# Casting the opening loads inside the DMA: matmul, GELU, matmul on one Trainium2 core

## The chip, the cores and the metric

The kernel runs on one core of a Trainium2 chip. A core has a matrix engine (TensorE, PE in the profile, with PEld for its weight loads), a vector engine (VectorE, DVE), a scalar engine (ScalarE, ACT), GpSimd (POOL) and a queue engine (SyncE, SP). Each engine works through its own list of instructions in order and waits for the others only through semaphores. Two lists issue loads here: SP's, whose transfers copy a type as it is, and POOL's, whose transfers may change the type on the way (float32 in the device memory, bf16 in the on-chip memory, SBUF). Both use the same 16 DMA engines. Matmul results land in PSUM, of which the kernel uses eight banks of 128 x 512 float32.

The metric is the device time of one execution in microseconds. Before the change the median of 13 executions is 124.84 us (124.44 to 125.33).

## The reference

```python
m, k, n, p = 1024, 1024, 2048, 1024      # a: m x k, b: k x n, c: n x p, all float32

def reference(a, b, c):
    h = np.matmul(a, b)
    h = 0.5 * h * (1 + np.tanh(np.sqrt(2 / np.pi) * (h + 0.044715 * h ** 3)))
    return np.matmul(h, c).astype(np.float32)
```

## The kernel before

The first product is computed transposed, so that its result can serve as the weights of the second. It is cut into 16 tiles of 128 columns of b (index t) and into two halves of 512 rows of a (index h). For one tile and one half eight matmuls (index k, 128 rows of b each) add up in one PSUM bank: weights are a 128 x 128 block of b, the moving operand is aT[h][:, k, :], 512 turned rows of a. ScalarE applies GELU from PSUM into the tiles hq (line 119). The second product is done in seven products of half matrices in place of eight (line 246), with sums and differences of the halves made by VectorE beforehand (s1, s2, s3, t1, t2, t3). The order of all work is the order in which the program is written.

What is loaded, and where:

- The opening block is 768 columns of b (tiles t = 0 to 5, W0) and the first half of a. SP loads both as float32: a_st (line 76; two slices of 128 columns, then three pairs) and b_st (line 82; eight slices, one for each k, 128 rows of 3072 bytes). SP's order is a slice, b slice, a slice, b slice, a pair, two b slices, and so on.
- For each k the loop at line 105 casts a_st to bf16 (ab, line 107, VectorE), turns it with four transposes on TensorE (line 110) into a bank of tpool, copies that to aT[0] (line 111, VectorE), casts b_st to b_lo with two ScalarE instructions (line 113), and issues the six matmuls of slice k - 1 (line 102).
- Tiles 6 to 9 (W1, 512 columns) come with two loads on POOL (load_b, line 126), each four slices of k, cast to bf16 on the way into b_lo. Ahead of them stands the gate (line 91), a copy of one column on POOL that reads slice 5 of b_st, so POOL issues nothing before that slice has landed. Here k is the outer loop: 32 matmuls (line 134) into four banks.
- Tiles 10 to 15 come into b_hi with four POOL loads, two k halves for 384 columns (W2) and two for the next 384. They run with t outside and k inside (mm1, line 143).
- The second half of a comes with four POOL loads (line 155), each 128 rows, cast to bf16. turn (line 158) makes eight transposes into a bank of tpool and one copy to aT[1] (line 163). turn(0) stands behind tile 13, turn(1) to turn(3) behind tile 14.
- c comes in eight POOL loads (line 188).

tpool has two banks, ppool six. The four tiles t1 take the buffers of a_st, the eight tiles t2 those of b_st (lines 195 and 196), and the partial results u2 those of the a1 slices.

Loads issued on POOL share eight semaphores in turn, so a load's issue waits until the eighth load before it on this queue has landed.

Of the kernel before, what the change touches and what calls it, by code (L numbers as in the profile page):

```python
# [19 lines left out]
def kernel(ctx, tc, a, b, c, out):  # L20
# [7 lines left out]
    H = 512  # L28
    N0 = 6
    W0 = N0 * 128  # L30
    N1 = 4
    W1 = N1 * 128

# [6 lines left out]
    keep = ctx.enter_context(tc.tile_pool(name="keep", bufs=1))  # L40
    astage = ctx.enter_context(tc.tile_pool(name="astage", bufs=4))
    abf = ctx.enter_context(tc.tile_pool(name="abf", bufs=4))
    b0stage = ctx.enter_context(tc.tile_pool(name="b0stage", bufs=8))
    opool = ctx.enter_context(tc.tile_pool(name="opool", bufs=4))
    ppool = ctx.enter_context(tc.tile_pool(name="ppool", bufs=6, space=PSUM))
    tpool = ctx.enter_context(tc.tile_pool(name="tpool", bufs=2, space=PSUM))

# [11 lines left out]
    def bcols(k0, kn, n0, w):  # L59
        if n0 < WB:  # L60
            return b_lo[:, k0:k0 + kn, ds(n0, w)]
        return b_hi[:, k0:k0 + kn, ds(n0 - WB, w)]

    def bt(k, t):
        return bcols(k, 1, t * 128, 128)[:, 0, :]
# [5 lines left out]

    a_st, b_st = {}, {}

    def load_a0(k, n):
        st = astage.tile([128, 4, 256], F32, name="a_st")
        nc.sync.dma_start(out=st[:, :, 0:n * 128], in_=av[:, 0:4, ds(k * 128, n * 128)])  # L76
        for i in range(n):
            a_st[k + i] = st[:, :, ts(i, 128)]

    def load_b0(k):  # L80
        st = b0stage.tile([128, W0], F32, name="b0_st")
        nc.sync.dma_start(out=st, in_=bv[:, k, 0:W0])  # L82
        b_st[k] = st

    gate = consts.tile([128, 1], F32, name="gate")
    for k, n in ((0, 1), (1, 1), (2, 2), (4, 2), (6, 2)):
        load_a0(k, n)
        for i in range(n):
            load_b0(k + i)

    nc.gpsimd.tensor_copy(gate, b_st[5][:, 0:1])
    g = consts.tile([128, 1], F32, name="g")
    nc.scalar.activation(g, warm[:, 0:1], AF.Gelu_apprx_tanh)
    wps = tpool.tile([128, H], F32, name="pt")
    for _ in range(10):
        nc.tensor.matmul(wps, warm[:, 0:128], warm, start=True, stop=True)

    ps = [ppool.tile([128, H], F32, name="ps") for _ in range(N0)]

    def mm0(k):  # L100
        for t in range(N0):
            nc.tensor.matmul(ps[t], bt(k, t), aT[0][:, k, :],  # L102
                             start=(k == 0), stop=(k == KT - 1))

    for k in range(KT):
        ab = abf.tile([128, 4, 128], BF16, name="ab")
        nc.vector.tensor_copy(ab, a_st[k])  # L107
        pt = tpool.tile([128, H], BF16, name="pt")
        for j in range(4):
            nc.tensor.transpose(pt[:, ts(j, 128)], ab[:, j, :], ident)  # L110
        nc.vector.tensor_copy(aT[0][:, k, :], pt)
        for i in range(2):
            nc.scalar.activation(b_lo[:, k, ts(i, W0 // 2)], b_st[k][:, ts(i, W0 // 2)], AF.Copy)  # L113
        if k > 0:
            mm0(k - 1)
    mm0(KT - 1)

    def gelu(t, h, p):
        nc.scalar.activation(hq[h][t // NH][:, t % NH, :], p, AF.Gelu_apprx_tanh)  # L119

    for t in range(N0):
        gelu(t, 0, ps[t])


    def load_b(k0, kn, n0, w):
        nc.gpsimd.dma_start(out=bcols(k0, kn, n0, w), in_=bv[:, k0:k0 + kn, ds(n0, w)])

    ps = [(tpool if t < 2 else ppool).tile([128, H], F32, name="pt" if t < 2 else "ps")
          for t in range(N1)]
    for k in range(0, KT, 4):  # L130
        load_b(k, 4, W0, W1)
        for i in range(4):
            for t in range(N1):
                nc.tensor.matmul(ps[t], bt(k + i, N0 + t), aT[0][:, k + i, :],  # L134
                                 start=(k + i == 0), stop=(k + i == KT - 1))
    for t in range(N1):
        gelu(N0 + t, 0, ps[t])


    def mm1(t, h):  # L140
        p = ppool.tile([128, H], F32, name="ps")
        for k in range(KT):
            nc.tensor.matmul(p, bt(k, t), aT[h][:, k, :],  # L143
                             start=(k == 0), stop=(k == KT - 1))
        gelu(t, h, p)

    W2 = 384
    for n0 in range(W0 + W1, N, W2):
# [9 lines left out]
    def turn(j):  # L158
        ab = a1[j]
        pt = tpool.tile([128, KT, 128], BF16, name="pt")  # L160
        for k in range(KT):
            nc.tensor.transpose(pt[:, k, :], ab[:, ts(k, 128)], ident)  # L162
        nc.vector.tensor_copy(aT[1][:, :, ts(j, 128)], pt)  # L163

    for t in range(N0 + N1, NT):
        mm1(t, 0)
        if t == NT - 3:
            turn(0)
        if t == NT - 2:
            turn(1)  # L170
            turn(2)
            turn(3)

# [20 lines left out]

    t1 = [astage.tile([128, 2, H], F32R, name="t1", tag="a_st") for _ in range(4)]
    t2 = [b0stage.tile([128, 1, H], F32R, name="t2", tag="b0_st") for _ in range(8)]
    s1 = keep.tile([128, NH, H], F32R, name="s1")
# [3 lines left out]

    def sum_t2(t):
        nc.vector.tensor_tensor(t2[t], c22[:, t:t + 1, :], t1[t // 2][:, t % 2:t % 2 + 1, :], op=SUB)

# [3 lines left out]
    for t in range(NT):  # L208
        mm1(t, 1)
        if 3 <= t < 7:  # L210
            sum_t1(t - 3)
        if 6 <= t < 10:
            sum_t2(2 * (t - 6))
            sum_t2(2 * (t - 6) + 1)
        if t == WB // 128:
            t3 = keep.tile([128, NH, H], F32R, name="t3", tag="B0")
        if t >= NH + 1:
            sum_s1(t - NH - 1)
        if WB // 128 <= t < WB // 128 + 4:
            i = t - WB // 128  # L220
            nc.vector.tensor_tensor(t3[:, ts(i, 2), :], c22[:, ts(i, 2), :], c12[:, ts(i, 2), :], op=SUB)
# [15 lines left out]

    def sum_t4(t):
        nc.vector.tensor_tensor(t2[t], t2[t], c21[:, t:t + 1, :], op=SUB)

# [8 lines left out]
    def whole(x):  # L249
        return lambda t: x[:, t, :]  # L250

    def halves(x):
        return lambda t: x[t // 4][:, t % 4, :]

    def pairs(x):
        return lambda t: x[t // 2][:, t % 2, :]

    def ones(x):
        return lambda t: x[t][:, 0, :]

# [26 lines left out]
    for j in R:  # L287
        p = bank()
        prod(p, halves(s2), ones(t2), j)
        nc.vector.tensor_tensor(u2[j], p, u2[j], op=ADD)  # L290
# [5 lines left out]
    for j in R:  # L296
        p = bank()
        prod(p, whole(s1), pairs(t1), j)
        combine(4 + j, 1, p, u3[:, j, :])
        nc.vector.tensor_tensor(u2[j], p, u2[j], op=ADD)  # L300
        sum_t4(2 * j)
        sum_t4(2 * j + 1)
    for j in R:
# [3 lines left out]
    for j in R:  # L307
        p = bank()
        prod(p, whole(h22), ones(t2), j)
        combine(4 + j, 0, p, u3[:, j, :], op=SUB, swap=True)  # L310
# [36 lines left out]
```

## Time and profile before

| What | Value |
|---|---|
| median of 13 executions | 124.84 us (124.44 to 125.33) |
| the profiled execution: its own time | 124.44 us |
| the profiled execution: its span | 122.7 us |
| PE busy | 114.8 us (94%), 555 instructions |
| DVE busy | 65.2 us (53%) |
| ACT busy | 29.6 us (24%) |
| POOL busy | 21.4 us (17%) |
| queue 0 (POOL's loads, "software_dynamic") | 7968 packets, 8.91 MB |
| queue 1 (SP's loads and stores, "hardware_dynamic") | 6240 packets, 9.44 MB |
| read from device memory, written to it | 20.97 MB, 4.19 MB |

The span runs from the first to the last instruction of the profiled execution; its own time is 1.7 us longer, for what lies around the program. The profile page cuts the span into 40 slices of 3.07 us. "Busy tenths" give the busy share of each engine in a slice, PEclk the clock granted to TensorE, GB/s what the DMA engines wrote: a load that casts float32 to bf16 writes half of what it reads. The chain of waits is followed backwards from the last instruction, at each step to what released it. In a timeline a row gives start, duration, engine, line, operation, output and input, count, and in brackets the idle time before it and what ended that.

### The profile page before, as it was taken

How to read it: one execution, taken by the hardware profiler on the slowest of the kernel's cores; microseconds unless marked ns; L12 is line 12 of the kernel's file. 1: busy time of each engine (PE TensorE's matmuls, PEld its weight loads, DVE VectorE, ACT ScalarE, POOL GpSimd, SP SyncE). 2: the span in 40 equal slices, each digit the busy share in tenths (PEclk: the TensorE clock that was granted, in tenths of full speed). 3: DMA queues.
4: the chain of work that ended last, by engine and by line, in shares of the span. 5: the costliest groups of instructions: out<-in, count | busy, mean ns of one | idle time of the engine just before them, and what ended most of it. 6: DMA issues, size and time to landing. Idle time of an engine off the chain costs nothing.

```text
span 122.7 us, 1436 instructions
## 1 busy us (share of the span) xinstructions
PE 114.8 (94%) x555; PEld 67.2 (55%) x562; DVE 65.2 (53%) x94; ACT 29.6 (24%) x54; POOL 21.4 (17%) x26
## 2 busy tenths in 40 slices
PE   6759989999998999999999999999999999999990
PEld 2224444444456444444444444468888888888860
DVE  0223543000014200007999999999769999964440
ACT  4054445806331133233332333000000000000000
POOL 2000099133440310000000000996000000000000
PEclk9977999999999999999999999999999999999999
DMA  2799999999999999996000000000600023353433
GB/s 92 213 368 380 377 303 198 206 201 202 211 206 206 322 397 234 206 206 100 0 3 0 5 0 0 0 0 25 232 0 0 5 86 120 137 199 143 171 143 114
DMA packets 14213, 18.43 MB, mean 150 GB/s; under 512 B 768, under 2 KB 9728, under 8 KB 14208
## 3 DMA queue, kind: packets, MB, share of 16 engines
q0 software_dynamic: 7968, 8.91, 39.3%
q1 hardware_dynamic: 6240, 9.44, 21.7%
q8 instruction: 4, 0.07, 0.2%
q14 instruction: 1, 0.01, 0.0%
HBM read 20.97 MB, written 4.19 MB: 205 GB/s over the span
## 4 chain that ended last, share of the span: by engine, by line
PE 82%; DMA 12%; DVE 1%; SPq 1%; issue 1%; DVEq 0%
PE ps L246 41%; PE ps L143 31%; DMA a_st<-in_a_dram 12%; PE ps L102 3%; PE ps L134 3%; PE pt L134 3%; PE pt L162 1%; DVE aT L163 1%; PE pt L110 1%; DVE ab L107 0%; SPq L82 0%; DVE ot L316 0%; SPq L76 0%; DVEq L107 0%
## 5 line engine op out<-in xcount | busy, mean ns | idle before, releaser
L119 ACT ACTIVATE h<-ps 128x512 fp32r<-128x512 f32 (+1 forms) x30 | 17.3, 601 | 27.5 <-PE ps L143 25.2
L143 PE MATMUL ps<-aT,b_hi 128*128 128x512 bf16 x93 | 21.2, 379 | 0.2
L143 PE MATMUL ps<-aT,b_lo 128*128 128x512 bf16 x79 | 17.4, 379 | 0.1
L143 PEld LDWEIGHTS <-b_hi 128*128 128x128 bf16 x96 | 9.3, 98 | 10.8
L246 PE MATMUL ps<-t,s 128*128 128x512 f32 x64 | 15.0, 392 | 0.0
L246 PE MATMUL ps<-t,h 128*128 128x512 f32 x64 | 14.8, 389 | 0.0
L246 PE MATMUL ps<-c,h 128*128 128x512 bf16 (+1 forms) x71 | 14.1, 355 | 0.1
L286 POOL COPY lk<-u 128x512 f32<-128x512 f32 x1 | 7.9, 7892 | 33.4 <-ACT u L279 33.4
L246 PEld LDWEIGHTS ps<-t,s 128*128 128x128 f32 x64 | 12.0, 188 | 2.6
L246 PEld LDWEIGHTS ps<-t,h 128*128 128x128 f32 x64 | 12.0, 188 | 2.5
L200 DVE TENSOR_TENSOR t<-c,c 128x1024 fp32r<-128x1024 bf16 x4 | 4.7, 1222 | 15.7 <-DMA c<-in_c_dram 15.4
L143 PEld LDWEIGHTS <-b_lo 128*128 128x128 bf16 x80 | 7.8, 98 | 9.4
L102 PE MATMUL ps<-aT,b_lo 128*128 128x512 bf16 x47 | 12.9, 414 | 0.1
L163 DVE COPY aT<-pt 128x1024 bf16<-128x1024 bf16 x4 | 2.7, 688 | 18.0 <-PE pt L162 17.9
L246 PEld LDWEIGHTS <-h 128*128 128x128 bf16 x72 | 6.9, 98 | 7.1 <-issue 0.3
L113 ACT ACTIVATE b_lo<-b_st 128x384 bf16<-128x384 f32 x16 | 7.5, 515 | 10.0 <-DMA b_st<-in_b_dram 9.8
L188 POOL DMA_DIRECT2D c<-in_c_dram x8 | 6.0, 745 | 12.4 <-DMA b_hi<-in_b_dram 5.7
L269 DVE TENSOR_TENSOR ot<-ps,u 128x512 f32<-128x512 f32 x11 | 7.3, 683 | 1.1 <-PE ps L246 1.1
L246 PE MATMUL ps<-c,s 128*128 128x512 f32 x32 | 7.4, 389 | 0.0
L102 PEld LDWEIGHTS <-b_lo 128*128 128x128 bf16 x48 | 4.8, 107 | 4.7 <-issue 1.3
L107 DVE CAST ab<-a_st 128x512 bf16<-128x512 f32 x8 | 3.7, 464 | 6.3 <-DMA a_st<-in_a_dram 6.3
L246 PEld LDWEIGHTS ps<-c,s 128*128 128x128 f32 x32 | 6.0, 188 | 1.2
(37 smaller groups left out, 89.8 us busy)
## 6 DMA issues: line engine op xcount, KB each, us to landing
out_dram<-ot SPq DMA_DIRECT2D x15, 256.0 KB, 2.0
b_st<-in_b_dram SPq DMA_DIRECT2D x8, 384.0 KB, 8.5
c<-in_c_dram POOLq DMA_DIRECT2D x6, 512.0 KB, 15.0
c<-in_c_dram POOLq DMA_DIRECT2D x2, 1024.0 KB, 15.0
a_st<-in_a_dram SPq DMA_DIRECT2D x3, 512.0 KB, 9.0
b_hi<-in_b_dram POOLq DMA_DIRECT2D x4, 384.0 KB, 11.4
b_lo<-in_b_dram POOLq DMA_DIRECT2D x2, 512.0 KB, 6.9
ab<-in_a_dram POOLq DMA_DIRECT2D x4, 256.0 KB, 14.1
```

The source lines that it names most:

```text
L102: nc.tensor.matmul(ps[t], bt(k, t), aT[0][:, k, :], start=(k == 0), stop=(k == KT - 1))
L107: nc.vector.tensor_copy(ab, a_st[k])
L113: nc.scalar.activation(b_lo[:, k, ts(i, W0 // 2)], b_st[k][:, ts(i, W0 // 2)], AF.Copy)
L119: nc.scalar.activation(hq[h][t // NH][:, t % NH, :], p, AF.Gelu_apprx_tanh)
L134: nc.tensor.matmul(ps[t], bt(k + i, N0 + t), aT[0][:, k + i, :], start=(k + i == 0), stop=(k + i == KT - 1))
L143: nc.tensor.matmul(p, bt(k, t), aT[h][:, k, :], start=(k == 0), stop=(k == KT - 1))
L163: nc.vector.tensor_copy(aT[1][:, :, ts(j, 128)], pt)
L188: nc.gpsimd.dma_start(out=dst[:, t:t + 4, :], in_=cv[:, r * NH + t:r * NH + t + 4, ts(q, H)])
L200: nc.vector.tensor_tensor(t1[i], c12[:, ts(i, 2), :], c11[:, ts(i, 2), :], op=SUB)
L246: nc.tensor.matmul(p, lhs(t)[:, ts(j, 128)], rhs(t)[:, q], start=(t == 0), stop=(t == NH - 1))
L269: nc.vector.tensor_tensor(ot, u if swap else p, p if swap else u, op=op)
L286: nc.gpsimd.tensor_copy(last_keep, last)
```

## The change

All loads but the first two a slices go to POOL and are cast inside the DMA. The opening order on POOL is b slice 0, b slice 1, then for each pair of k an a pair and two b slices; b slices go straight into b_lo, so b0stage and ScalarE's casts are gone, and VectorE casts only the first two a slices. The gate goes. The loads of b_lo's second block and of b_hi follow on the same queue, and b_hi now comes in two loads of 768 columns (one for each k half), since W2 is the whole rest.

In the opening loop the transposes and the copy of slice k + 1 stand between the third and fourth matmul of slice k. All transposes of the opening go through one PSUM bank cut in two (pts); ppool has seven banks, tpool one. The turns of the second half of a take banks of ppool and are placed inside tiles: turn(0) behind tile 13, turn(1) after four matmuls of tile 14, turn(2) behind it, turn(3) after four matmuls of tile 15. t1 and t2 get buffers of their own; t2 is four tiles of 128 x 1024, and the sums on it are done in four instructions in place of eight. NB equals N0, so the loop over range(NB, N0) is empty.

```diff
     N0 = 6
+    NB = 6
...
+    KG = 4
...
-    astage = ctx.enter_context(tc.tile_pool(name="astage", bufs=4))
+    astage = ctx.enter_context(tc.tile_pool(name="astage", bufs=2))
     abf = ctx.enter_context(tc.tile_pool(name="abf", bufs=4))
-    b0stage = ctx.enter_context(tc.tile_pool(name="b0stage", bufs=8))
...
-    ppool = ctx.enter_context(tc.tile_pool(name="ppool", bufs=6, space=PSUM))
-    tpool = ctx.enter_context(tc.tile_pool(name="tpool", bufs=2, space=PSUM))
+    ppool = ctx.enter_context(tc.tile_pool(name="ppool", bufs=7, space=PSUM))
+    tpool = ctx.enter_context(tc.tile_pool(name="tpool", bufs=1, space=PSUM))
...
-    def load_a0(k, n):
-        st = astage.tile([128, 4, 256], F32, name="a_st")
-        nc.sync.dma_start(out=st[:, :, 0:n * 128], in_=av[:, 0:4, ds(k * 128, n * 128)])
...
-    def load_b0(k):
-        st = b0stage.tile([128, W0], F32, name="b0_st")
-        nc.sync.dma_start(out=st, in_=bv[:, k, 0:W0])
-        b_st[k] = st
-
-    gate = consts.tile([128, 1], F32, name="gate")
-    for k, n in ((0, 1), (1, 1), (2, 2), (4, 2), (6, 2)):
-        load_a0(k, n)
-        for i in range(n):
-            load_b0(k + i)
-
-    nc.gpsimd.tensor_copy(gate, b_st[5][:, 0:1])
+    def load_b(k0, kn, n0, w):
+        nc.gpsimd.dma_start(out=bcols(k0, kn, n0, w), in_=bv[:, k0:k0 + kn, ds(n0, w)])
+
+    a_bf = {}
+    a_st = []
+    for k in range(2):
+        st = astage.tile([128, 4, 128], F32, name="a_st")
+        nc.sync.dma_start(out=st, in_=av[:, 0:4, ts(k, 128)])
+        a_st.append(st)
+    load_b(0, 1, 0, W0)
+    load_b(1, 1, 0, W0)
+    for k in range(2, KT, 2):
+        st = abf.tile([128, 4, 256], BF16, name="ab", tag="ab1")
+        nc.gpsimd.dma_start(out=st, in_=av[:, 0:4, ds(k * 128, 256)])
+        for i in range(2):
+            a_bf[k + i] = st[:, :, ts(i, 128)]
+            load_b(k + i, 1, 0, W0)
...
-    for k in range(KT):
-        ab = abf.tile([128, 4, 128], BF16, name="ab")
-        nc.vector.tensor_copy(ab, a_st[k])
-        pt = tpool.tile([128, H], BF16, name="pt")
+    def turn0(k):
+        if k < 2:
+            ab = abf.tile([128, 4, 128], BF16, name="ab0", bufs=2)
+            nc.vector.tensor_copy(ab, a_st[k])
+        else:
+            ab = a_bf[k]
+        pt = pts[:, k % 2, :]
         for j in range(4):
             nc.tensor.transpose(pt[:, ts(j, 128)], ab[:, j, :], ident)
         nc.vector.tensor_copy(aT[0][:, k, :], pt)
-        for i in range(2):
-            nc.scalar.activation(b_lo[:, k, ts(i, W0 // 2)], b_st[k][:, ts(i, W0 // 2)], AF.Copy)
-        if k > 0:
-            mm0(k - 1)
-    mm0(KT - 1)
+
+    turn0(0)
+    for k in range(KT):
+        for t in range(NB):
+            nc.tensor.matmul(ps[t], bt(k, t), aT[0][:, k, :],
+                             start=(k == 0), stop=(k == KT - 1))
+            if t == 2 and k + 1 < KT:
+                turn0(k + 1)
...
-    def mm1(t, h):
+    def mm1(t, h, between={}):
         p = ppool.tile([128, H], F32, name="ps")
         for k in range(KT):
             nc.tensor.matmul(p, bt(k, t), aT[h][:, k, :],
                              start=(k == 0), stop=(k == KT - 1))
+            for x in between.get(k, ()):
+                turn(x)
         gelu(t, h, p)
...
-    W2 = 384
+    W2 = N - W0 - W1
     for n0 in range(W0 + W1, N, W2):
         for k in range(0, KT, 4):
             load_b(k, 4, n0, W2)
...
     def turn(j):
-        ab = a1[j]
-        pt = tpool.tile([128, KT, 128], BF16, name="pt")
+        pt = ppool.tile([128, KT, 128], BF16, name="pt", tag="ps")
         for k in range(KT):
-            nc.tensor.transpose(pt[:, k, :], ab[:, ts(k, 128)], ident)
+            nc.tensor.transpose(pt[:, k, :], a1[j][:, ts(k, 128)], ident)
         nc.vector.tensor_copy(aT[1][:, :, ts(j, 128)], pt)
 
+    turns = {NT - 3: {7: [0]}, NT - 2: {3: [1], 7: [2]}, NT - 1: {3: [3]}}
     for t in range(N0 + N1, NT):
-        mm1(t, 0)
-        if t == NT - 3:
-            turn(0)
-        if t == NT - 2:
-            turn(1)
-            turn(2)
-            turn(3)
+        mm1(t, 0, turns.get(t, {}))
...
-    t1 = [astage.tile([128, 2, H], F32R, name="t1", tag="a_st") for _ in range(4)]
-    t2 = [b0stage.tile([128, 1, H], F32R, name="t2", tag="b0_st") for _ in range(8)]
+    t1 = [keep.tile([128, 2, H], F32R, name=f"t1{i}") for i in range(4)]
+    t2 = [keep.tile([128, 2, H], F32R, name=f"t2{i}") for i in range(4)]
...
-    def sum_t2(t):
-        nc.vector.tensor_tensor(t2[t], c22[:, t:t + 1, :], t1[t // 2][:, t % 2:t % 2 + 1, :], op=SUB)
+    def sum_t2(i):
+        nc.vector.tensor_tensor(t2[i], c22[:, ts(i, 2), :], t1[i], op=SUB)
```

## The prediction

> **What bounds the kernel now.** I read the page first: the chain that ended last, then the busy tenths.
>
> ```profile
> PEclk9977999999999999999999999999999999999999
> DMA  2799999999999999996000000000600023353433
> GB/s 92 213 368 380 377 303 198 206 201 202 211 206 206 322 397 234 206 206 100 0 3 0 5 0 0 0 0 25 232 0 0 5 86 120 137 199 143 171 143 114
> ...
> PE 82%; DMA 12%; DVE 1%; SPq 1%; issue 1%; DVEq 0%
> ```
>
> TensorE carries the chain, loads some 15 us of it (12% of 122.7). The DMA engines are full from slice 2 to slice 17: 370 to 380 GB/s for float32 into float32, about 206 GB/s written for float32 into bf16, which reads twice that. A cast in the DMA therefore costs no read rate in steady flow. Next I read the chain in order of time and the timeline around its turning points.
>
> ```profile
> 7.03 9.80 DMA a_st<-in_a_dram
> ...
> 17.49 0.40 PE pt L110 x4
> ...
> 38.47 0.70 DVE aT L163
> ```
>
> ```profile
> 7.75 2.77 PE L102 MATMUL ps<-aT,b_lo 128*128 128x512 bf16 x6
> ...
> 15.69 1.46 PE L102 MATMUL ps<-aT,b_lo 128*128 128x512 bf16 x6
> ...
> 21.70 6.71 PEld L134 LDWEIGHTS <-b_lo 128*128 128x128 bf16 x32 [0.20 <-DMA b_lo<-in_b_dram]
> ...
> 28.74 3.62 PE L143 MATMUL ps<-aT,b_hi 128*128 128x512 bf16 x16
> ...
> 39.21 0.61 PE L162 MATMUL pt<-ident,ab 128*128 128x128 bf16 x8 [0.34 <-DVE aT L163]
> ```
>
> The opening waits for loads until 17.49. From there TensorE has work to the end, but for one break at L162. The two six-matmul lines are the same work at 7.75 and at 15.69, in 2.77 and 1.46 us: the first ran at half clock. Last, when loads land. A POOL load waits for the eighth before it, so POOL's timeline dates the landings:
>
> ```profile
> 15.55 1.63 POOL L126 DMA_DIRECT2D b_lo<-in_b_dram  x2
> 17.17 2.98 POOL L126 DMA_DIRECT2D b_hi<-in_b_dram  x4
> ...
> 21.95 0.54 POOL L155 DMA_DIRECT2D ab<-in_a_dram  x1 [0.71 <-DMA b_lo<-in_b_dram]
> ...
> 27.14 0.75 POOL L188 DMA_DIRECT2D c<-in_c_dram  x1 [2.11 <-DMA b_hi<-in_b_dram]
> 29.03 0.75 POOL L188 DMA_DIRECT2D c<-in_c_dram  x1 [1.14 <-DMA b_hi<-in_b_dram]
> ...
> 32.98 0.74 POOL L188 DMA_DIRECT2D c<-in_c_dram  x1 [1.27 <-DMA b_hi<-in_b_dram]
> ...
> 35.42 0.74 POOL L188 DMA_DIRECT2D c<-in_c_dram  x1 [0.46 <-DMA ab<-in_a_dram]
> ```
>
> The first b_lo load had landed at 21.95, the four b_hi loads at 27.14, 29.03, 30.97 and 32.98, the second a1 slice at 35.42. TensorE starts b_hi at 28.74 and needs its second k half four matmuls later, at 29.60 (a matmul takes 0.216: 32 of L134 in 6.9 us). That load was 0.57 us early. So behind a TensorE without gaps the queue runs almost level with it. An earlier TensorE gains nothing unless the loads come earlier too.
>
> **The change, part by part.** *Opening loads.* SP issues 2 loads instead of 13. POOL issues 11 more, then the rest as before. By POOL's rows a 128-row load costs 0.54 (a1, L155) and a 512-row load 0.75 (L126, L188): 8 x 0.54 + 3 x 0.75 = 6.6 us on an engine that waited 14.1 us for the gate copy, which goes. POOL's setup ends at 1.31, so I put the first issue at 1.3. From the ninth load on, each waits for the eighth before it, and the a1 slices from the second on also for TensorE to have turned the buffer's slices. Eight loads in flight hold over 1.5 MB written, over 7 us of transfer at 206 GB/s, so the queue does not run dry.
>
> When do they land? From 21.95 (512 KiB written since the first issue) to 35.42 (3072 KiB) are 13.47 us for 2560 KiB: 5.26 us per 1000 KiB. The first load took 21.95 - 15.55 = 6.40, of which 2.69 by this rate; 3.71 is start and lag of the slowest engine. In the new order the sums written are: eight opening b slices and three a pairs 1536 + 768 = 2304 KiB, b_lo's two loads 512 each (2816, 3328), b_hi's two 768 each (4096, 4864). So landings are 1.3 + 3.71 + 5.26 per 1000 KiB: last b slice 17.1, b_lo 19.8 and 22.5, b_hi 26.6 and 30.6. Its other bound is the full window rate, 206 GB/s: 4864 KiB take 24.2, so 29.2; POOL's release also comes a little after the landing. Between 29.2 and 30.6 I take 30.2, nearer the slope, as it is measured on landings. The hardware queue's two a slices (256 KiB each) go before the first cast load's data and are not added. The 512-byte rows of the a pairs are in no row of before; the nearest, 768-byte rows, ran at 200 GB/s as against 206. For 768 KiB that is 0.1 us, at twice the difference 0.2: inside the choice.
>
> The Trainium skill, page "DMA: Bandwidth & Descriptors", section "Latency and other measured facts", speaks against the move: it gives the software path about 1 us to the first byte and the hardware path about 0.6. Here the first hardware load was cast 2.9 us after its issue, and the software path's 3.71 above holds its share already; the page alone would add 0.4 us to the opening and leave the other terms.
>
> *Casts.* ScalarE's 16 (515 ns) and six of VectorE's eight go. In the middle both lay under loads; at the end of the opening two of ScalarE's (1.0 us) stood between the last slice and its matmuls. The opening: last slice 17.1, six matmuls 1.3, end 18.4 if the clock is full; with the half-clock stretch of before (1.31 extra in six matmuls, some 1.7 in all) eight slices of 1.5 us, from the first b slice at 1.3 + 3.71 + 1.0 = 6.0 on, end at 19.7. Either way b_lo's first load (19.8) decides, against 21.8 before: 2 us gained here. VectorE's copy of a turned slice (0.42) now has three matmuls (0.65) to hide under.
>
> *b_hi in two loads of 768 columns instead of four of 384.* Here the gain ends. The first three of the six column tiles no longer have loads of their own: the second k half of all six must be there at the first tile's fifth matmul. TensorE: 19.8 + 6.9 + 0.86 = 27.6. The load: 30.2. TensorE stalls 2.6 us, and resumes at 30.2 where it had been at 29.60: +0.6. Queued behind it is everything TensorE does; the a1 slices (1.3 us each after it) land by 35.6, and the first is turned at 30.2 + 0.86 + 3 x 1.72 = 36.2, so no load is late next.
>
> *Turns.* Before, 24 transposes took 37.82 to 39.66, 1.84 us, where 24 at 0.44 per eight need 1.32: 0.52 stall, since the PSUM pair was full. In the new order each turn has its own bank. The last one's copy ends 0.95 after its transposes (36.09 to 36.99, and a release of 0.05), over four matmuls of 0.86: 0.09 stall. Net -0.43.
>
> *Sums, banks, tiles of t2.* Four sums of 1216 ns for eight of 684, twice. VectorE does them far from TensorE's need, and L246 had no wait for a bank: nothing. Without that cover the change would gain 8 x 0.684 - 4 x 1.216 = 0.6 us in each place, not lose it.
>
> *The clock.* A 2.6 us stall has its nearest row in the opening:
>
> ```profile
> 5.00:5.50 0.50, 0.22 (x4) 0.04 (x1) 0.25 (x1) 0.00 (x0) 0.00 (x0) 1.00 0.71 179
> ...
> 7.00:7.50 0.50, 0.04 (x1) 0.04 (x2) 0.40 (x1) 0.09 (x1) 0.00 (x0) 1.00 0.95 289
> ...
> 8.00:8.50 0.50, 0.50 (x2) 0.15 (x1) 0.42 (x1) 0.07 (x1) 0.00 (x0) 0.50 1.10 391
> ...
> 10.50:11.00 0.50, 0.50 (x6) 0.46 (x6) 0.00 (x0) 0.10 (x1) 0.00 (x0) 0.50 1.03 369
> ```
>
> Columns: window, length, busy time of PE, PEld, DVE, ACT, POOL, granted clock, DMA share, GB/s. TensorE sat idle from 5.2 to 7.46, 2.2 us; from 7.6 to 11.0 its clock was 0.5. So 3.4 us at half speed, 1.7 us lost. The 0.5 us gap at 17.0 cost nothing. Bounds for 2.6 us: 0 and 1.7. I take 1.4: the gap is longer than the one that did it, and part of the slow stretch may fall into the stall.
>
> The skill's page "TensorE: Matmul & The Clock Gate", section "Part 1: The HAM clock gate", says the clock halves after at least one idle window of about 3.4 us, free-running: by that, 2.6 us would not suffice and the sum loses this term. The row shows 2.2 us sufficing once.
>
> *Sum.* +0.6 - 0.43 + 1.4 = +1.6. On the profiled execution: span 122.7 to 124.3, time 124.44 to 126.0. That execution is the fastest of the 13, 0.40 under their median of 124.84; against the median the sum is 126.4.
>
> **Rivals.** *Stall without slow clock.* For: the 0.5 us gap cost nothing, no row tells where between 0.5 and 2.2 the loss begins or whether it always comes, and the landing may be earlier. Against: the 2.2 us gap. 124.84 + 0.6 - 0.43 = 125.0; with the landing at 29.9 to 30.8, 124.7 to 125.6.
>
> *The queue keeps window rate: faster.* Place: b_hi's second load. Landing 29.2 by 206 GB/s, and 0.35 earlier as a 128-row first load issues in 0.54 instead of 0.88: 28.85, stall 1.3, too short for the clock. 124.84 + (28.85 - 29.60) - 0.43 = 123.7. It decides from a landing before about 29.8. For: full windows before. Against: the slope of the landings, which holds the slowest engine.
>
> *A slow start.* From 2 to 6 us the loads of before moved 0.9 MB, 224 GB/s where later they ran at 385: 1.7 us lost. Cast loads, whose data start near 3.2 (before, they began 1.9 after their issue at 15.55: the window 17.5 to 18.0 fell to 102 GB/s between SP's last and POOL's first), would meet 2.8 of these 4 us; if they run as badly there, all landings move 1.2 us: 126.4 + 1.2 = 127.6. Against: part of it may be SP's own issue, which spread to 10.2 us.
>
> *The change doesn't do what it says:* the order of POOL's instructions in the changed kernel has the 11 loads ahead of the rest, with the waits named above, so this is out.
>
> **How the numbers follow.** Forecast 0.40 (its own range 125.7 to 127.2); stall without slow clock 0.27; faster queue 0.23; slow start 0.10. A measurement of this kernel tells about 0.2%, 0.25 us, from no change: 124.59 to 125.09. Of the second case half lies inside this band, 0.14; the rest is slower. Faster 0.24, with a hundredth from the second case's early end; same 0.14; slower 0.62. The range takes the faster case's centre and stops short of the slow start: 123.7 to 127.3.
>
> **What would show it.** A TensorE gap of 2 to 3 us before the fifth matmul on b_hi, ended by a b_hi load near 30.2, and a half-clock stretch behind it; b_lo's first weights near 19.8; no wait at L162 over 0.1; DMA full from 3.5 us on. A b_hi landing under 29.5, or full clock behind the gap, makes the forecast wrong.

## The result, and the profile after

The changed kernel takes 126.65 us (median of 11 executions, 125.77 to 129.19); the kernel before took 124.92 beside it (48 executions, 124.17 to 125.87). The ratio is 1.0127, with a 95% interval from 1.010 to 1.0154: slower by some 1.6 us. The medians here are of all executions, while each ratio leaves out those that took over 1.5% more than the fastest of the same kernel, so a ratio can lie nearer to 1 than its two medians do. The times of the changed kernel spread more than those before: six lie at or under 126.65, five between 127.55 and 129.19. Its profiled execution took 126.75 with a span of 124.9, where the one before took 124.44 with a span of 122.7.

The page of the changed kernel, busy tenths in 40 slices (3.12 us each) and the chain that ended last by engine:

```profile
PE   6939999999799999999999999999999999999980
PEclk9999999999999999999999999999999999999999
DMA  3899999999999999990000000006000023353442
GB/s 97 132 162 202 202 206 206 210 210 211 209 204 240 399 309 206 206 163 13 0 0 0 5 0 0 0 0 252 3 0 0 5 84 117 134 203 132 168 159 93
...
PE 71%; DMA 21%; POOL 3%; issue 1%; DVE 1%; POOLq 0%
```

Loads now carry 21% of the chain where they carried 12%. Casting loads write at 202 to 211 GB/s from the fourth slice to the twelfth, but the second and third, from 3.1 to 9.4 us, reach only 132 and 162, though the DMA engines are 80% busy or more there. The chain in order of time (start, length, what) has b_hi's second load as its turning point:

```profile
4.42 9.41 DMA ab<-in_a_dram
...
14.11 0.74 POOL b_hi L74
...
15.06 16.95 DMA b_hi<-in_b_dram
32.01 0.04 issue
32.05 5.57 PE ps L129 x25
```

TensorE's timeline of the same execution (start, length, what, count, and in brackets the idle time before and what ended it):

```profile
8.33 1.46 PE L114 MATMUL ps<-aT,b_lo 128*128 128x512 bf16 x3 [2.26 <-DMA b_lo<-in_b_dram]
...
10.01 2.77 PE L114 MATMUL ps<-aT,b_lo 128*128 128x512 bf16 x6
...
15.02 1.49 PE L114 MATMUL ps<-aT,b_lo 128*128 128x512 bf16 x6
...
23.17 7.17 PE L143 MATMUL ps<-aT,b_lo 128*128 128x512 bf16 x31
30.18 1.03 PE L129 MATMUL ps<-aT,b_hi 128*128 128x512 bf16 x4
32.05 6.22 PE L129 MATMUL ps<-aT,b_hi 128*128 128x512 bf16 x27 [0.85 <-DMA b_hi<-in_b_dram]
...
43.43 1.90 PE L129 MATMUL ps<-aT,b_lo 128*128 128x512 bf16 x8
```

Four matmuls on b_hi start at 30.18, the fifth waits for the second k half until 32.05. The four take 0.87, so TensorE was ready at 31.05 and lost 1.0. What follows runs at full clock (25 matmuls in 5.57). Before, the fifth matmul on b_hi ran at 29.60: it is now 2.45 late. From there to the first tile of the second half are 11.38 us (32.05 to 43.43), where there were 11.78 (29.60 to 41.38): the turns give back 0.40. The sum, +2.05, stands against a span longer by 2.2.

POOL's timeline dates the landings, since each of its loads waits for the eighth before it:

```profile
8.57 0.76 POOL L86 DMA_DIRECT2D ab<-in_a_dram  x1 [2.30 <-DMA b_lo<-in_b_dram]
...
24.33 0.75 POOL L183 DMA_DIRECT2D c<-in_c_dram  x1 [1.39 <-DMA b_lo<-in_b_dram]
28.58 0.74 POOL L183 DMA_DIRECT2D c<-in_c_dram  x1 [3.50 <-DMA b_hi<-in_b_dram]
32.29 0.74 POOL L183 DMA_DIRECT2D c<-in_c_dram  x1 [2.97 <-DMA b_hi<-in_b_dram]
```

The first b slice landed by 8.57, b_lo's second load by 24.33, b_hi's two by 28.58 and 32.0. From the second of these to the last are 1536 KiB in 7.7 us, or 204 GB/s: the steady rate. The time was lost earlier; windows of 1 us (the last columns are granted clock, DMA share and GB/s) show where:

```profile
4.00:5.00 1.00, 1.00 (x3) 0.30 (x2) 0.18 (x1) 0.00 (x0) 1.00 (x2) 1.00 0.58 78
5.00:6.00 1.00, 1.00 (x6) 0.52 (x4) 0.00 (x0) 0.00 (x0) 1.00 (x3) 1.00 1.06 94
6.00:7.00 1.00, 0.07 (x1) 0.00 (x0) 0.76 (x2) 0.00 (x0) 0.27 (x1) 1.00 0.99 98
7.00:8.00 1.00, 0.00 (x0) 0.00 (x0) 0.00 (x0) 0.00 (x0) 0.00 (x0) 1.00 1.18 154
8.00:9.00 1.00, 0.67 (x2) 0.28 (x3) 0.00 (x0) 0.00 (x0) 0.43 (x1) 1.00 1.31 199
```

From 4 to 8 us 424 KB were written, where the rate from 8 us on (about 202) makes 808: 384 KB short, or 1.9 us. The DMA share is full from 5 us on all the same.

### The profile page after: what moved, and what is told of

It reads as the page before. It is cut to its first block, busy times and chain, and to the rows that moved or that the text cites. A ratio compares the mean times of both kernels' runs of the same rounds, so it can differ in the third digit from the quotient of the medians.

```text
span 124.9 us, 1390 instructions
## 1 busy us (share of the span) xinstructions
PE 116.6 (93%) x555; PEld 68.0 (54%) x562; DVE 62.5 (50%) x80; ACT 22.1 (18%) x38; POOL 23.1 (18%) x34
## 4 chain that ended last, share of the span: by engine, by line
PE 71%; DMA 21%; POOL 3%; issue 1%; DVE 1%; POOLq 0%
PE ps L240 40%; PE ps L129 29%; DMA b_hi<-in_b_dram 14%; DMA ab<-in_a_dram 8%; POOL b_lo L74 2%; PE pt L162 1%; POOL ab L86 1%; POOL b_hi L74 1%; DVE aT L163 1%; DVE ot L306 0%; POOL ident masks.py:199 0%; POOL ident masks.py:197 0%; POOLq masks.py:199 0%; POOLq L321 0%
## 5 line engine op out<-in xcount | busy, mean ns | idle before, releaser
L120 ACT ACTIVATE h<-ps 128x512 bf16<-128x512 f32 (+1 forms) x32 | 18.2, 601 | 51.4 <-PE ps L129 24.9
L129 PE MATMUL ps<-aT,b_lo 128*128 128x512 bf16 x79 | 17.4, 379 | 0.2
L114 PE MATMUL ps<-aT,b_lo 128*128 128x512 bf16 x47 | 14.1, 439 | 2.3 <-DMA b_lo<-in_b_dram 2.3
L277 POOL COPY lk<-u 128x512 f32<-128x512 f32 x1 | 4.6, 4623 | 33.5 <-ACT u L270 33.5
L109 DVE COPY aT<-pts 128x512 bf16<-128x512 bf16 x8 | 3.4, 425 | 13.9 <-PE pts L108 13.9
L143 PE MATMUL ps<-aT,b_lo 128*128 128x512 bf16 x31 | 7.1, 379 | 0.1
```

The costliest lines, as they stand in the source:

```text
L114: nc.tensor.matmul(ps[t], bt(k, t), aT[0][:, k, :], start=(k == 0), stop=(k == KT - 1))
L129: nc.tensor.matmul(p, bt(k, t), aT[h][:, k, :], start=(k == 0), stop=(k == KT - 1))
L143: nc.tensor.matmul(ps[t], bt(k, N0 + t), aT[0][:, k, :], start=(k == 0), stop=(k == KT - 1))
L277: nc.gpsimd.tensor_copy(last_keep, last)
```

## Experiments

All kernels of one group shared their runs of the kernel before, whose median was 124.8 in the first group, 124.78 in the second, 124.79 in the third and 125.08 in the fourth, which is the last kernel below alone.

**Fine b_hi loads in the changed kernel.**

```diff
-    W2 = N - W0 - W1
+    W2 = 384
```

> The changed kernel with b_hi in four loads of 384 columns again (W2 = 384). In the profiled changed kernel TensorE reached b_hi's fifth matmul at 31.05 and its load let it go at 32.05. With 384 columns the loads that tile 10 needs are written 768 KiB earlier, at 5 us per 1000 KiB some 4 us. Theory A, the late second b_hi load decides: the wait before the fifth matmul goes, TensorE runs on from 30.2, 1.0 us less: 125.6, and in executions with a shorter opening more. Rival B, the opening's end and the slow clock behind it decide everywhere: no change by more than the wait's own 1.0, and the opening still ends near 23 us. Rival C, the coarse load is hidden: 126.65.

Measured: 124.35 (10 executions), ratio 0.9952 (0.9909 to 0.9996). TensorE's timeline of this kernel:

```profile
21.19 7.08 PE L143 MATMUL ps<-aT,b_lo 128*128 128x512 bf16 x31 [0.44 <-DMA b_lo<-in_b_dram]
28.11 7.07 PE L129 MATMUL ps<-aT,b_hi 128*128 128x512 bf16 x31
```

No wait stands at b_hi any more: it starts at 28.11 and runs on through its fifth matmul. Undoing this one line takes 2.3 us off the changed kernel (126.65 to 124.35), all of the loss and a little more. That is more than the wait of 1.0 in the profiled execution of the changed kernel. Part of the rest is that the opening ended earlier here (21.19 for 23.17), which the coarse loads would have turned into a longer wait.

**The opening loads back on SP**, in float32 with staging, casts and the gate, and with the eight small t2 tiles; the coarse b_hi loads and the new turns stay.

```diff
-    load_b(0, 1, 0, W0)
-    load_b(1, 1, 0, W0)
-    for k in range(2, KT, 2):
...
+    for k, n in ((0, 1), (1, 1), (2, 2), (4, 2), (6, 2)):
+        load_a0(k, n)
+        for i in range(n):
+            load_b0(k + i)
+
+    nc.gpsimd.tensor_copy(gate, b_st[5][:, 0:1])
```

> The changed kernel with the opening loads on SP as before (float32, staging, casts on ScalarE and VectorE, the gate, eight tiles t2), the rest as changed, b_hi in two loads of 768 columns. Theory A, the landing of b_hi's second load decides: in the kernel before, the same 5.24 MB had landed by 32.98, so TensorE is let go near 32.8 against 32.05 in the changed kernel: 126.65 + 0.75 = 127.4, up to 1.7 more where the clock falls in a wait of 3 us. Rival B, the move of the opening loads to POOL is the cause: near the time before less 0.4 for the turns, 124.5.

Measured: 128.13 (4 executions), ratio 1.0187 (1.0097 to 1.0277). TensorE's timeline of this kernel:

```profile
33.01 6.22 PE L135 MATMUL ps<-aT,b_hi 128*128 128x512 bf16 x27 [2.68 <-DMA b_hi<-in_b_dram]
39.06 0.61 PE L168 MATMUL pt<-ident,ab 128*128 128x128 bf16 x8
```

With the old opening b_hi's second half comes at 33.01, a microsecond later than in the changed kernel, and the kernel is slower than it, by 1.5 us in the medians and by 0.7 in the ratios (1.0187 and 1.0127, whose intervals overlap). So the move to POOL is not what costs; given the coarse loads it gains, if anything. The 28 matmuls behind the 2.68 us wait took 6.05 (33.01 to 39.06), full clock: a wait of this length need not slow it.

**Eighteen warming matmuls for ten**, so that TensorE works until the first b slice is there. (These are matmuls on zeros ahead of the real work, whose results nothing reads.)

```diff
-    for _ in range(10):
+    for _ in range(18):
```

> The changed kernel with 18 warming matmuls in place of 10, so that TensorE's idle time from 6.1 to 8.3 us shrinks and the opening runs at full speed. Theory A: the opening ends some 2.5 us earlier, near 20.5, and the wait for b_hi's second load grows by as much: TensorE is let go at 32.05 as before, 126.65, or 1 to 1.7 more where the longer wait slows the clock. Rival B, the slow opening decides: 2.5 us less, 124.2.

Measured: 127.47 (4 executions), ratio 1.0172 (1.0082 to 1.0261). TensorE's timeline, then windows, of the profiled execution, which was the longest of the four (128.13):

```profile
21.68 7.08 PE L143 MATMUL ps<-aT,b_lo 128*128 128x512 bf16 x31 [0.49 <-DMA b_lo<-in_b_dram]
...
31.74 7.90 PE L129 MATMUL ps<-aT,b_hi 128*128 128x512 bf16 x27 [2.12 <-DMA b_hi<-in_b_dram]
39.48 0.61 PE L162 MATMUL pt<-ident,ab 128*128 128x128 bf16 x8
```

```profile
32.00:33.00 1.00, 1.00 (x6) 0.45 (x5) 0.00 (x0) 0.19 (x1) 0.71 (x1) 1.00 1.12 209
33.00:34.00 1.00, 1.00 (x4) 0.41 (x3) 0.00 (x0) 0.41 (x1) 0.74 (x1) 0.54 1.12 209
...
35.00:36.00 1.00, 1.00 (x4) 0.32 (x3) 0.00 (x0) 0.20 (x1) 0.19 (x1) 0.50 1.19 205
```

The opening ends 1.5 us earlier than in the changed kernel's profile (21.68 for 23.17), and the fifth matmul on b_hi is let go at 31.74, almost where it was (32.05): the landing decides, and what the opening gains is only waited for there. Behind the wait the granted clock falls to 0.50, and 28 matmuls take 7.74 where they took 6.05 in the experiment above: 1.7 us lost.

**Both of these edits.**

```diff
-    for _ in range(10):
+    for _ in range(18):
...
-    W2 = N - W0 - W1
+    W2 = 384
```

> Both edits: b_hi in loads of 384 columns, 18 warming matmuls. Theory A: the opening ends near 20.5, b_hi's first two loads have landed by 28.1, tile 10 starts near 27.5 and its fifth matmul near 28.2, against 29.60 in the kernel before; with 0.4 from the turns 124.9 - 1.4 - 0.4 = 123.1, faster than both kernels. Rival B, either edit alone has the whole effect: the same time as the better of the two alone. Rival C, loads land later than the changed kernel's profile shows: a wait of over 1 us at b_hi, about 124.5.

Measured: 123.62 (123.08 to 123.88 in 4 executions), ratio 0.9897 (0.9837 to 0.9957). With the fine loads the warming now helps, by 0.7. Tile 6 starts at 21.39, after 0.41 of waiting for b_lo, and b_hi has no wait. In the profiled execution with fine loads alone (123.6) tile 6 started as early, at 21.19; the other executions of that kernel reach 124.88. It is likely that the warming removes a half-speed opening from some executions, but those were not profiled. Each execution's mean granted clock fits this: it is 0.996 to 1.0 in the four with warming, and 0.986 or less in six of the ten with fine loads alone, which took 123.98 to 124.88.

**The kernel before with the coarse b_hi loads alone.**

```diff
-    W2 = 384
+    W2 = 768
```

> The kernel before with one edit: b_hi in two loads of 768 columns (W2 = 768). Theory A, the late second b_hi load is what the change loses by: the load ends with the same last byte as the fourth load of 384 columns did, whose landing let POOL go at 32.98; TensorE wants it at 29.60, so it waits some 3.2 us: 124.8 + 3.2 = 128.0, up to 1.7 more in executions where the clock falls after the wait. Rival B, the coarse load costs only together with the software queue's opening: 124.8.

Measured: 128.84 (4 executions), ratio 1.0291 (1.0233 to 1.035). TensorE's timeline, then windows, of its profiled execution (129.54, the longest of its times):

```profile
29.52 1.04 PE L143 MATMUL ps<-aT,b_hi 128*128 128x512 bf16 x4
33.21 7.70 PE L143 MATMUL ps<-aT,b_hi 128*128 128x512 bf16 x28 [2.65 <-DMA b_hi<-in_b_dram]
40.75 0.61 PE L162 MATMUL pt<-ident,ab 128*128 128x128 bf16 x8
```

```profile
33.00:34.00 1.00, 0.79 (x2) 0.28 (x3) 0.00 (x0) 0.00 (x0) 0.55 (x1) 0.50 1.12 209
...
36.00:37.00 1.00, 1.00 (x5) 0.43 (x4) 0.00 (x0) 0.00 (x0) 0.74 (x1) 0.88 1.21 205
```

This one line costs the old kernel 4.06 us in the medians and 3.6 by the ratio. In the profile the fifth matmul on b_hi goes from 29.60 to 33.21, +3.6, and the clock behind the 2.65 us wait is 0.50: 28 matmuls in 7.54, 1.5 lost. Together 5.1, which is what the span grew by (122.7 to 127.8).

**The kernel before with the new turns alone** (in the two banks of tpool).

```diff
+    turns = {NT - 3: {7: [0]}, NT - 2: {3: [1], 7: [2]}, NT - 1: {3: [3]}}
     for t in range(N0 + N1, NT):
-        mm1(t, 0)
...
+        mm1(t, 0, turns.get(t, {}))
```

> The kernel before with one edit: the turns of the second half of a spread as in the changed kernel (turn(0) behind tile 13, turn(1) after four matmuls of tile 14, turn(2) behind it, turn(3) after four matmuls of tile 15), in the two banks they had. Theory A: the 0.5 us break goes and 0.1 comes: 124.8 - 0.4 = 124.4. Rival B, the break was covered by something else: 124.8.

Measured: 124.39 (12 executions), ratio 0.9966 (0.994 to 0.9993), a gain of 0.39.

In the medians the parts add up: 124.8 + 4.06 (coarse loads) - 0.39 (turns) - 1.48 (opening on POOL, 126.65 against 128.13) = 126.99, with 126.65 measured. By the ratios the three are 3.6, 0.4 and 0.7, and the sum is 127.3 for 126.4, so the agreement is to about 1 us. And the opening on POOL with fine loads (124.35) is not to be told from the old opening with the same turns (124.39).

**b_lo's second block in loads of two k slices**, with both edits above.

```diff
-    KG = 4
+    KG = 2
```

> b_hi in loads of 384 columns and 18 warming matmuls (123.62 so far), and b_lo's second block in four loads of two k slices each (KG = 2). TensorE waited at 21.39 for b_lo's first load of four k slices; half of it is there 256 KiB or 1.3 us sooner. Theory A, landings set the end of the opening: tile 6 starts near 20.5, where the opening ends, and everything after it 0.8 us earlier: 122.8. Rival B, b_hi's loads then come too late: a wait at the fifth matmul of tile 10 takes part of it back, 123.3. Rival C, no effect: 123.6.

Measured: 123.47 (6 executions), ratio 0.9891 (0.9854 to 0.9927). Tile 6 starts at 20.45 and b_hi at 27.45, and TensorE shows no gap from 8.33 on. The gain over 123.62 is inside the spread of both.

**The first two b loads ahead of the building of the identity**, on the kernel just above.

```diff
-    make_identity(nc, ident)
...
     load_b(1, 1, 0, W0)
+    make_identity(nc, ident)
```

> As the run with KG = 2, and POOL issues its first two b loads ahead of the identity matrix, 0.7 us earlier. Theory A, the software queue's slow start is a stretch of fixed length after its first issue: all landings 0.6 us earlier, 122.3, less where TensorE's own work sets the opening's end. Rival B, the slow start is tied to the time since the program began and not to the first issue (the loads on SP were slow until 6 us too): landings hardly move, 122.8.

Measured: 123.18 (6 executions), ratio 0.9864 (0.9823 to 0.9904). POOL's first issue came at 1.24 for 1.43, only 0.2 earlier: inconclusive. The profile named a new wait, though. The first slice's matmuls came at 8.94, behind the last warming matmul, the transposes queued after it and VectorE's copy of them.

**Eight of the 18 warming matmuls behind the first turn**, so that the copy is hidden under them.

```diff
-    for _ in range(18):
+    for _ in range(10):
         nc.tensor.matmul(wps, warm[:, 0:128], warm, start=True, stop=True)
...
     turn0(0)
+    for _ in range(8):
+        nc.tensor.matmul(wps, warm[:, 0:128], warm, start=True, stop=True)
```

> As the run with KG = 2 and the first two b loads ahead of the identity matrix, with the 18 warming matmuls split: 10 ahead of the first turn, 8 behind it, so that the first turned slice does not wait for all of them. There the first real matmul ran at 8.94, after the last warming matmul, a turn and a copy, while the first b slice had landed near 7. Theory A: the first matmul runs near 7.5, and as TensorE has no gap from there to the end in that run, all of it moves: 123.2 - 1.4 = 121.8. Rival B, the loads behind it are late then (b_lo's first load landed near 18.9, the opening would end near 19.6; b_hi's second near 26.8, wanted near 27.4): 122.5.

Measured: 122.8 (122.46 to 123.3 in 5 executions), ratio 0.9844 (0.981 to 0.9878). This beats both kernels, the one before by 2.0 us. TensorE's timeline of it:

```profile
5.47 1.89 PE L113 MATMUL ps<-warm 128*128 128x512 bf16 x8
7.19 0.81 PE L116 MATMUL ps<-aT,b_lo 128*128 128x512 bf16 x3
...
20.09 7.17 PE L145 MATMUL ps<-aT,b_lo 128*128 128x512 bf16 x32
27.10 7.07 PE L131 MATMUL ps<-aT,b_hi 128*128 128x512 bf16 x32
```

The first real matmul runs at 7.19 and at full clock (three in 0.81), and tile 6 at 20.09 for 23.17 in the changed kernel. Theory A's 121.8 was not reached: the first matmul came 1.75 earlier than in the kernel just above, tile 6 only 0.96 (20.09 for 21.05), and at 17.24 TensorE waited 0.25 for a load of b_lo.

**Why the queue starts slowly.** Three runs on the version with loads of two k slices asked what the slow stretch belongs to. First, SP loads 64 bytes of each row of b into a tile that nobody reads, so that those rows have been touched before.

```diff
+    touch = consts.tile([128, KT, 16], F32, name="touch")
+    nc.sync.dma_start(out=touch, in_=bv[:, :, 0:16])
```

> As the run with KG = 2, plus one load of 64 bytes from each of b's 1024 rows on SP, ahead of POOL's first, into a tile that nothing reads. In all runs so far the DMA engines wrote some 100 to 125 KB/us of cast data from 3.5 to 7 us and 205 after, and the loads on SP before were as slow over the same microseconds. Theory A, the first touch of b's rows is what is slow: the rate is 205 from 4 us on, the last opening slice lands 1.3 us earlier. Rival B, the start of the program is slow, whatever was touched: landings as in the run with KG = 2, or later by the extra load's transfer, and 123.5.

Measured: 123.01 (4 executions), ratio 0.9855 (0.9826 to 0.9884). The rates in the four windows from 4 to 8 us were 100, 107, 141 and 162 GB/s, much as without it (125, 92, 136, 166). But the touching load itself moved between 5 and 8 us, beside POOL's first loads, so this run tells nothing.

Second, POOL's first load is held until the second a slice has landed.

```diff
+    gate = consts.tile([128, 1], F32, name="gate")
+    nc.gpsimd.tensor_copy(gate, a_st[1][:, 0, 0:1])
```

> As the run with KG = 2, with POOL's first load held back until SP's second a slice has landed, some 2.5 us later (a copy of one column on POOL). Theory A, the slow stretch belongs to the time since the program began (until about 7 us): only what was moved in the lost time is lost, some 230 KiB, so the opening's last slice lands 1.2 us later and the time is 124 to 125. Rival B, the slow stretch follows the first issue on this queue: everything lands 2.5 us later, and the rate is under 125 KB/us until 9.5 us.

Measured: 125.71 (4 executions), ratio 1.0072 (1.0043 to 1.01). Windows of it:

```profile
6.00:7.00 1.00, 1.00 (x8) 0.50 (x6) 0.00 (x0) 0.00 (x0) 1.00 (x2) 1.00 1.08 117
7.00:8.00 1.00, 0.03 (x1) 0.00 (x0) 0.84 (x2) 0.00 (x0) 1.00 (x3) 1.00 0.70 109
...
9.00:10.00 1.00, 1.00 (x9) 0.61 (x8) 0.14 (x1) 0.00 (x0) 1.00 (x2) 1.00 0.72 87
...
11.00:12.00 1.00, 0.74 (x3) 0.13 (x3) 0.00 (x0) 0.00 (x0) 0.53 (x1) 1.00 1.26 200
```

The first issue came at 4.62 for 1.43, and the slow stretch moved with it: 87 to 125 GB/s from 6 to 10 us, 168 in the window after, 184 to 207 from 11 on. It belongs to the queue's first loads and not to a time in the program. It isn't a sharing with the a slices either, which had landed by then.

Third, the same hold, with the touching load done before it ends.

```diff
+    touch = consts.tile([128, KT, 16], F32, name="touch")
+    nc.sync.dma_start(out=touch, in_=bv[:, :, 0:16])
+    gate = consts.tile([128, 1], F32, name="gate")
+    nc.gpsimd.tensor_copy(gate, a_st[1][:, 0, 0:1])
```

> As the run with POOL's first load held back, plus the 64-byte touch of each of b's rows on SP behind the a slices. In the run with the touch alone its 64-byte packets moved from 5 to 8 us, together with POOL's first loads, so it could not be ahead of them; here POOL's data start near 6 and the touch has 4 to 6 us to itself. Theory A, the first touch of b's rows is slow: the touch takes its time from 4 to 6 us and POOL's first loads then run at 205 KB/us instead of the 117, 109, 125 and 87 of the delayed run; the opening's last slice lands some 1.5 us earlier. Rival B, the first loads on the queue are slow whatever was touched: the rates and landings of the delayed run, 125.7.

Measured: 125.8 (8 executions), ratio 1.0068 (1.0023 to 1.0112). Windows of it:

```profile
7.00:8.00 1.00, 1.00 (x7) 0.47 (x6) 0.00 (x0) 0.00 (x0) 1.00 (x3) 1.00 1.13 117
...
10.00:11.00 1.00, 0.86 (x5) 0.21 (x3) 0.42 (x1) 0.00 (x0) 0.55 (x1) 1.00 0.93 120
11.00:12.00 1.00, 0.63 (x3) 0.10 (x1) 0.00 (x0) 0.00 (x0) 0.53 (x1) 1.00 1.34 198
```

The rows had been touched, and the stretch is as slow as before. So what makes it slow is not that b's rows are read for the first time, as far as 64 bytes of each row can show that. Nor does the queue need so long whatever it starts with. In the kernel before its first loads have 512 rows and are issued at 15.55, and after SP's last data the windows read:

```profile
18.00:19.00 1.00, 1.00 (x6) 0.36 (x5) 0.92 (x2) 0.97 (x3) 1.00 (x2) 1.00 1.08 176
19.00:20.00 1.00, 1.00 (x9) 0.64 (x9) 0.42 (x1) 0.73 (x2) 1.00 (x2) 1.00 1.24 197
```

One window below the steady rate, at 176, and then 197. So the long stretch goes with a start on loads of 128 rows, though loads of that size run at some 202 GB/s from 8 us on.

The traces show two things more. The packets themselves are slower: in the changed kernel those of 1536 bytes took 275, 235 and 177 ns on average in the windows from 5, 6 and 7 us, and 134 from 9 us on, so the engines are busy at a low rate. And the stretch ends within 2 us of the last load that POOL issues without a pause (6.27 in the changed kernel, 10.21 and 10.55 in the two that hold POOL's first load). So POOL's own issuing of one 128-row load after another is a rival that no run tests. No run opened the changed kernel with larger loads either, so why the first ones are slow stays open.

## Why the prediction came out right, and where its steps did not

It said 126.4, and 126.65 was measured. Its main step holds: the coarse b_hi loads turn the gain of the opening into a wait at the fifth matmul on b_hi. The old kernel with that one line lost 4.06 us in the medians, and the changed kernel without it lost nothing. But two terms of the sum were wrong by similar amounts in opposite directions: the landing cost 1.85 more than predicted, the clock 1.4 less. That the total came within 0.25 is luck. By the prediction's own signs it was wrong in the profiled execution: the wait was 1.0 us where it said 2 to 3, and the clock behind it was full. That execution looks like the rival "stall without slow clock" with a later landing: 124.84 + 2.45 - 0.43 = 126.9.

*Landing of b_hi's second load: mis-sized.* Predicted 30.2 (+0.6 for TensorE), measured 32.0 (+2.45). The step that failed is the start term. By the full rate 4864 KiB take 24.2 us; from the first issue at 1.43 to 32.0 that leaves 6.4 for start and lag of the slowest engine, where 3.71 was taken from the first load of the kernel before, a start with 512-row loads that had only one slow window. Of the 6.4, some 2.6 passed until SP's two a slices were through at about 4.0 (the windows from 2 to 4 us wrote 252 and 260 KB, about their 512 KiB). In the kernel before, POOL's data began 1.9 after its first issue, and 1.4 after it in the kernel that holds POOL's first load (4.62, nothing written until 6.0), so SP's slices cost 0.7 or more, which the prediction put at nothing. Another 1.9 are the slow stretch. The rest, 1.9, I put down to the lag of the slowest engine, without a run of its own; 3.71 less its 1.9 leaves about as much. The slope went the other way: 5.0 us per 1000 KiB from b_lo's second landing to b_hi's second. The prediction chose 30.2 near its bound of 5.26, and the other bound, 4.97 by 206 GB/s, was the right one: over 4864 KiB that is 1.4 us less, which made up for half of the 2.7 by which the start was too short (6.4 for 3.71).

*The slow-start rival was there.* It priced itself at 1.2 us for all landings, and the stretch cost 1.9. It got a chance of 0.10 because a part of the early loss was laid at SP's issues; the two kernels that hold POOL's first load show that these loads on POOL have such a stretch of their own, after SP has finished too. Its sum, 127.6, kept the clock term of 1.4; without it and with 1.9 for 1.2 it is 126.9. "DMA full from 3.5 us on" was right by the busy share from 5 us on and wrong by what was written.

*The opening: wrong, and without effect.* First matmul 8.33 for the predicted 6.0, end of the opening 23.17 for 18.4 to 19.7, b_lo's first weights at 22.96 rather than at 19.8. So nothing was gained here in that execution (tile 6 started at 21.83 before). "Either way b_lo's first load decides" failed in it, since half speed from 8.33 to about 14 (six matmuls in 2.77 at 10.01, in 1.96 at 13.00) held TensorE beyond b_lo's landing; where TensorE was kept warm, b_lo did decide, at 21.39 and 21.68. It cost the total little, as the wait at b_hi shrank by what the opening lost: 1.0 instead of 2.6.

*The clock: +1.4 predicted, 0 in the profiled execution.* The wait there was too short to be the one that was predicted. Where waits had about the predicted length, the loss came twice in three profiles: 1.7 behind 2.12 us, 1.5 behind 2.65, nothing behind 2.68. So the term is real, with 1.7 as the upper bound that was given, but it is paid in some executions only.

What decides can be read from the traces. In each of the 14 profiles the clock changes only at whole steps of 3.41 us from its first change (in the kernel before at 4.20, 7.61 and 11.02). Here are the steps that hold the three waits: one with 18 warming matmuls, one of the kernel before with coarse loads, and two with the opening on SP, where a step ends inside the wait. The first number behind the comma is TensorE's busy time in the step, the third from the end the clock.

```profile
29.67:33.08 3.41, 1.34 (x7) 0.64 (x8) 0.00 (x0) 0.81 (x3) 0.74 (x1) 1.00 1.12 209
29.42:32.83 3.41, 1.14 (x6) 0.31 (x4) 0.00 (x0) 1.67 (x4) 0.74 (x1) 1.00 1.14 211
28.14:31.55 3.41, 1.91 (x9) 0.50 (x6) 0.00 (x0) 2.06 (x4) 0.74 (x1) 1.00 1.15 210
31.55:34.96 3.41, 1.95 (x9) 0.90 (x10) 0.00 (x0) 0.60 (x1) 1.21 (x2) 1.00 1.12 209
```

TensorE was busy for 1.34 and 1.14 us of the first two, and the whole step behind each ran at 0.50. The wait of 2.68 is shared by two steps with 1.91 and 1.95 us of work, and the clock stayed full. The other steps agree. Half clock followed 1.17, 1.18 and 1.34 us of work in three openings (kernel before, the same with coarse loads, opening on SP); a full clock stayed full after 1.65 (kernel before with the new turns), 1.70 (fine loads) and every step with more. So the work within a step counts, and not the length of the wait alone, and where the steps fall decides whether a wait of 2 to 3 us is paid for twice. No run moved a wait against the steps on purpose.

The term can explain the five times from 127.55 up, which were not profiled; that is argued, not shown. Their mean granted clocks, 0.967 to 0.982, are lower than those of five of the six shorter ones (0.982 to 0.994), but the sixth, 126.6, has 0.968. Two experiments fit better: with 18 warming matmuls the execution at 1.0 took 126.0 and the three at 0.98 to 0.986 took 127.39 to 128.13; in the kernel before with coarse loads it is 127.46 at 1.0 and 128.79 to 129.54 at 0.973.

The Trainium skill's page "TensorE: Matmul & The Clock Gate", section "Part 1: The HAM clock gate", has the clock halve after at least one idle window of about 3.4 us that runs freely. The steps of 3.41 us fit such a window. But it need not be idle throughout: 1.34 us of work in a step did not keep the clock, and a wait of 2.12 us was enough, so here the measurement decides.

*Turns: right.* -0.43 predicted, -0.40 in the profile, -0.39 for the turns alone. No wait stood at L162.

*Casts and sums at nothing:* no wait of TensorE on either is in the profile after.

## What to carry to other kernels

When a queue is the bound and its consumer runs level with it, the size of a load sets when its first byte can be used: loads twice as wide cost 3.6 to 4.1 us at an unchanged rate, part of it by a slower clock, since three tiles had to wait for data that only the other three needed. A gain ahead of such a point is worth nothing until that point is moved: the warmer opening gave nothing (127.47) with wide b_hi loads and 0.7 us with narrow ones. Price the start of a queue by a start with loads of the same shape, and where no row has one, widen the bound.

## What the hardware showed that I had not expected

The first 4 us of data on POOL's queue are written at 78 to 154 GB/s, against some 202 to 206 later, while the DMA engines show a full share for most of it; the stretch follows the queue's first issue (from 6 us on when that came at 4.62), whether or not each row has been touched before, and is short (one window at 176) where the queue opens with 512-row loads.

Whether a wait slows TensorE depends on steps of 3.41 us that run on whatever the program does: of a step with 1.34 us of work or less the next ran at half clock, while 1.65 us kept it full. Two waits of 2.65 and 2.68 us ended differently for that reason.

A row of full granted clock doesn't prove full clock. In the changed kernel's profile six matmuls at 10.01 took 2.77 and six at 15.02 took 1.49, and the clock of this window reads 1.00 (the third number from the end):

```profile
10.00:10.50 0.50, 0.50 (x5) 0.23 (x3) 0.24 (x1) 0.00 (x0) 0.04 (x1) 1.00 1.18 204
```

The trace's first entry on the clock comes at 14.00, just where the matmuls turn fast, and the rows ahead of it read 1.00 without one. The spacing of equal matmuls is the safer reading.
